# Beginning weight pairs two at a time, in one PSUM bank a pair, and more of them

## The chip, the cores and the metric

The kernel runs on one core of one Trainium2 chip. The metric is the device time of one execution in microseconds (us). The engines of the core each take their own instructions in order: PE (TensorE, matrix products), ACT (ScalarE), DVE (VectorE), POOL (GpSimd) and SP (SyncE, which here only issues transfers). Products are written to PSUM, in banks of 128 x 512 floats, and are read from there by ACT and DVE; everything else lies in SBUF.

## The reference, cut to what matters

One layer of a diffusion backbone over 1024 latent tokens and 256 context tokens, with 1024 channels, in float32:

```
x  = x  + 0.5*g1 * swiglu(modulate(rms_norm(x)),  ffn1_w_in, ffn1_w_out)    # first half step
cx = cx + 0.5*g1c* swiglu(modulate(rms_norm(cx)), ffn1_w_in, ffn1_w_out)
hx = modulate(rms_norm(x));  hc = modulate(rms_norm(cx))
bg, cg, vc, q, k, v, gates = split(hx @ w_in)          # the mixers (1024 x 6656)
y  = bg * short_conv(cg * vc)                          # three taps along the tokens
o  = attention(q, [k_ctx, k], [v_ctx, v])              # 8 query heads, 2 key heads
x  = x + g5 * ((sig(gc)*(y @ w_bc) + sig(ga)*(o @ w_ba)) @ w_out)
x  = x + 0.5*g8 * swiglu(modulate(rms_norm(x)), ffn2_w_in, ffn2_w_out)      # second half step
out = rms_norm(x)

swiglu(h, w_in, w_out): a, b = split(h @ w_in, 2);  (silu(a) * b) @ w_out   # 1024 x 5632, 2816 x 1024
```

The two places of this text are the product `hx @ w_in` of the mixers and the product `h @ ffn2_w_in` of the second half step.

## The kernel before, in words

**Products.** Every float32 product is made of three matmuls on a 128 x 128 weight tile and a 128 x 512 tile of activations: both operands are split into a high part, rounded to the type fp32r, and a low part, the rest. ACT makes the high part (a cast), DVE subtracts it for the low part: this is `split` (lines 197 to 203). The three matmuls are high x high, high x low, low x high (`terms`, lines 688 to 693).

**Seven products for eight.** The large products with two column blocks at once, a *pair* of 128 columns each, go through a Strassen-Winograd scheme (class `Winograd`, lines 492 to 792). Activations are halved by channels and by tokens (C0 is the first 512 tokens, C1 the last), weights by rows and by the two columns of the pair. Seven products of half size (four 128-row tiles of depth, so 4 x 3 = 12 matmuls each) replace eight. Products 1 and 2 need only the halves of C0 (tiles named r, kept under `self.r[1]` and `self.r[2]`) and the first column's own weights; their sum is c, the first one alone is u. Products 6, 7, 4, 5 and 3 need sums of halves, so also C1 (`self.r[3]` to `self.r[7]`), and sums of weights, which GpSimd makes (`lefts`, tiles named sum). DVE adds them to u and c step by step (`second`, `third`).

**Norms.** `norm0` (line 530) norms and modulates C0 and writes r[1] and r[2]. `norm1` (line 557) does C1 and makes the differences: for each of four k it runs six tensor operations and five splits on DVE, and seven operations on ACT. It is a generator, run in six steps: the root mean square, its broadcast, and one step for each k.

**Beginning pairs ahead.** C1 is normed last, and PE would stand still in that time. So `start` (line 710) computes products 1 and 2 of the first `n_ahead` pairs beforehand: 9 for the mixers (AH2) and 9 for the second half step (AH3, line 47). For each pair, product 1 goes to a PSUM bank, ACT copies it to u (a tile named uc), a step of `norm1` is run, product 2 goes to another bank, DVE adds it to u for c, and SP stores u and c to DRAM (tiles named ucd), `put_aside`. The main loop fetches them again one pair ahead (`fetch`), and goes on with products 6, 7, 4, 5 and 3. A pair that wasn't begun has all seven products in the main loop. For a begun pair the weights of its first column are loaded once more in the main loop, for the sums.

**Buffers.** PSUM: five banks for these products (`ps_s`). SBUF: three tiles for raw weights ("raw"), four for split weights ("wl"), four under the tag "wh", which the uc tiles of `start` and the weight sums of the main loop share (`W_BUFS`), eleven small ones for u, c, v, b and the like.

**Look-ahead.** `left` (line 684) makes sure before each product that four split weights are ready or queued in the program (`prefetch`), and takes the first.

**The order of the work.** The program's order is not the order of an engine's queue. The framework plans each engine's order when the kernel is built: an instruction is put in its queue when the planner's own model has its inputs and its buffer ready, the earlier in the program first. Only instructions pinned by hand (`pinned`, `strict`) keep their place. On the chip each engine then waits for whatever stands at the head of its queue.

**Around the change.** For the mixers, `mix.prefetch(4)` and `mix.start(norm1)` stand after the row products of the first half step (lines 1324 to 1329); the main loop over the columns (lines 1346 to 1369) then mixes products with the convolution on DVE, the norm of the context (`normc2`) and the modulation (`mix_steps`). For the second half step, `fast.start(fast.norm1())` stands at line 1816, followed by the loop over 22 pairs.

Of the kernel before, what the change touches and what calls it, by code (L numbers as in the profile page):

```python
# [9 lines left out]
F32 = mybir.dt.float32  # L10
# [8 lines left out]
P = 128  # L19
# [19 lines left out]
W_BUFS = 4  # L39
# [4 lines left out]
WAIT = 4  # L44
AH1, BY_HALF, WARM = 13, 8, 32
TOKENS_AT = 5
RESIDENT, AH2, AH3 = 2, 9, 9
SLOT = 1024


# [1 line left out]
def tile_dit_layer(  # L52
# [44 lines left out]
    act, dve, pool, pe, sp = (Engine(e) for e in (nc.scalar, nc.vector, nc.gpsimd, nc.tensor, nc.sync))  # L97
# [3 lines left out]
    wpool = ctx.enter_context(tc.tile_pool(name="wpool", bufs=5))  # L101
# [7 lines left out]
    def uniq(s):  # L109
        n_tiles[0] += 1  # L110
        return f"{s}_{n_tiles[0]}"

    def atile(name, shape=(P, SLOT), dt=F32):
        return apool.tile(list(shape), dt, tag="A", name=uniq(name))
# [8 lines left out]
    def ps_s(n=512):  # L123
        return psum.tile([P, 512], F32, tag="s", name=uniq("ps"), bufs=5)[:, :n]
# [7 lines left out]
    def matmul(out, w, x, start, stop, pinned=False, on=False):  # L132

        inst = pe.matmul(out, w, x, start=start, stop=stop, skip_group_check=on)
        if pinned:
            tc.keep_in_program_order(inst)
# [49 lines left out]
    def col(name, k=0):  # L186
        o = voff[name] + k
        return cols[:, o : o + 1]
# [36 lines left out]
    def load_cols(w, o, lo_eng=None, pinned=False):  # L225

        return load_w(w[:, o : o + P].rearrange("(k p) n -> p k n", p=P), (KD, P), lo_eng, pinned)

    def mm3(ps, terms, k0=0, k1=None):

        last = len(terms) - 1
        for i, (wh, wl, xh, xl) in list(enumerate(terms))[k0:k1]:
            matmul(ps, wh, xh, start=(i == 0), stop=False)
            matmul(ps, wh, xl, start=False, stop=False)
            matmul(ps, wl, xh, start=False, stop=(i == last))
# [230 lines left out]
    def run(steps, n=None):  # L466

        if n is None:
            for _ in steps:
                pass  # L470
        else:
            for _ in range(n):
                next(steps, None)
# [18 lines left out]
    class Winograd:  # L492
# [192 lines left out]
            self.prefetch(4)  # L685
            return self.ready.pop(0)

        def terms(self, ps, w, i, k):
            r = self.r[i][k]
            wh, wl = (w[:, v, k * P : (k + 1) * P] for v in range(2))  # L690
            matmul(ps, wh, r[:, 0], start=k == 0, stop=False)
            matmul(ps, wh, r[:, 1], start=False, stop=False)
            matmul(ps, wl, r[:, 0], start=False, stop=k == 3)

        def product(self, i):
            w, ps = self.left(), ps_s()
# [12 lines left out]

        def start(self, norm):  # L710

            for i in range(self.n_ahead):
                t = wpool.tile([P, 2, 512], F32, tag="wh", name=uniq("uc"), bufs=W_BUFS)
                u, c = t[:, 0], t[:, 1]
                act.copy(out=u, in_=self.product(1))
                run(norm, 1)
                dve.tensor_add(out=c, in0=u, in1=self.product(2))
                self.put_aside(t)
            run(norm)
            self.fetch()  # L720

# [369 lines left out]
    for k in range(4):  # L1091
        if k % 2:
            half1.shifted(h0[k][:, 0], k, xh[k])
        else:
            dve.tensor_scalar(
                out=h0[k][:, 0], in0=xh[k], scalar1=gain1["l"][:, k : k + 1], scalar2=modl[:, k : k + 1],
                op0=ALU.mult, op1=ALU.add,
            )
        half1.keep(1, k, h0[k][:, 0])
    start = half1.start_by_half()  # L1100
    run(start, 1)
    for k in range(4):
        xt = turned(t0, k + 4, ps_o if k % 2 else ps_t)
# [46 lines left out]
    def all_later_mods():  # L1150
        yield from later_mod(1, (1,), (1,))
        yield from later_mod(0, (0, 1), (1,))
        part_gain(gain1["c"], 0, "g1", "c", 0, 8)
        for _ in normc:
            yield
        for m in range(2, 5):
            yield from later_mod(m)

    steps = all_later_mods()
# [66 lines left out]
    for j in range(NH):  # L1226
        half1.side = side(j) if j >= SIDE_FROM else None
        u, c = half1.next_first()
# [117 lines left out]
    for i in range(KD):  # L1346
        u = atile("u")
# [5 lines left out]
        for ch, bg, gc in mixed():  # L1353
# [4 lines left out]
            for j in (0, 2):  # L1358
# [3 lines left out]
                    out=ya, in0=u[:, a + j - 1 : b + j - 1], scalar=col(f"w{j}", i), in1=ya, op0=ALU.mult, op1=ALU.add  # L1362
# [325 lines left out]
    u = units[0]  # L1688
# [57 lines left out]
    for ch in (C0, C1):  # L1746
        o = ch[1]
        for d in range(KD):
            w = load_cols(w_out[0], d * P)
            load(xs(d, ch), xd[d, :, o : o + 512])  # L1750
            ps = ps_s()
# [4 lines left out]
                out=xs(d, ch), in0=ps, scalar=modl[:, 40 + d : 41 + d], in1=xs(d, ch), op0=ALU.mult, op1=ALU.add  # L1756
# [12 lines left out]
        out=gf[:], in0=cols[:, voff["gf"] : voff["gf"] + 8], scalar1=math.sqrt(D), scalar2=None, op0=ALU.mult  # L1769
# [47 lines left out]
    for j in range(NH):  # L1817
        if j > 1:
            run(last_steps, 3)
        u, c = fast.next_first()  # L1820
# [82 lines left out]
```

## Time and profile before

| | |
|---|---|
| median of three runs | 2644.59 us (2644.15 to 2645.6) |
| the profiled execution: time | 2648.45 us |
| its span, first to last instruction | 2646.7 us |
| granted TensorE clock, mean | 0.994 |
| busy: PE, DVE, ACT, POOL | 2620.2, 2019.7, 1173.9, 549.7 us |
| matmuls | 12665 |

The rows below are from the profile of that execution. "out<-in" names the tiles that an instruction writes and reads; all instructions stand under line 90, where a helper issues them, so they are told apart by tiles. The end of a matmul in the profile is modelled, so a busy PE isn't PE at its peak: counts of matmuls in a stretch of time say more. A number behind "<-" is the idle time of an engine and what ended it.

### The profile page before, as it was taken

How to read it: one execution, taken by the hardware profiler on the slowest of the kernel's cores; microseconds unless marked ns; L12 is line 12 of the kernel's file. 1: busy time of each engine (PE TensorE's matmuls, PEld its weight loads, DVE VectorE, ACT ScalarE, POOL GpSimd, SP SyncE). 2: the span in 40 equal slices, each digit the busy share in tenths (PEclk: the TensorE clock that was granted, in tenths of full speed). 3: DMA queues.
4: the chain of work that ended last, by engine and by line, in shares of the span. 5: the costliest groups of instructions: out<-in, count | busy, mean ns of one | idle time of the engine just before them, and what ended most of it. 6: DMA issues, size and time to landing. Idle time of an engine off the chain costs nothing.

```text
span 2646.7 us, 35358 instructions
## 1 busy us (share of the span) xinstructions
PE 2620.2 (99%) x12665; PEld 2180.4 (82%) x12665; DVE 2019.7 (76%) x3382; ACT 1173.9 (44%) x2321; POOL 549.7 (21%) x425
## 2 busy tenths in 40 slices
PE   8999999999999999999999999999999999999998
PEld 6888898888888777888888888888887888888888
DVE  5888876888897898877788676685457876666996
ACT  6533454433554632333355576674235333334553
POOL 0144101221010044332023112141001442321100
PEclk9999999999999999999999999999999999999999
DMA  8666465335973455242522532123525542327831
GB/s 322 203 211 195 140 214 168 113 120 204 319 170 115 136 171 169 98 133 78 204 73 91 88 88 64 33 49 105 161 81 178 185 155 86 98 76 281 197 84 64
DMA packets 367018, 378.40 MB, mean 143 GB/s; under 512 B 19431, under 2 KB 252025, under 8 KB 366841
## 3 DMA queue, kind: packets, MB, share of 16 engines
q1 hardware_dynamic: 357400, 357.22, 41.7%
q0 software_dynamic: 9440, 18.91, 4.3%
q8 instruction: 99, 1.62, 0.3%
q14 instruction: 79, 0.64, 0.1%
HBM read 306.26 MB, written 69.76 MB: 142 GB/s over the span
## 4 chain that ended last, share of the span: by engine, by line
PE 59%; DVE 2%; ACT 1%; issue 1%; DMA 0%; POOL 0%; SPq 0%; DVEq 0%; ACTq 0%; POOLq 0%
PE ps L90 49%; PE po L90 5%; PE pt L90 5%; DVE xb L90 0%; DVE y L90 0%; DVE r L90 0%; DMA c<-ucd 0%; DVE wl L90 0%; DVE rs_t L90 0%; ACT r L90 0%; DVE wc L90 0%; ACT pts L90 0%; POOL sum L90 0%; DVE pts L90 0%; ACT q L90 0%
## 5 line engine op out<-in xcount | busy, mean ns | idle before, releaser
L90 PE MATMUL ps<-r,wl 128*128 128x512 f32 x5196 | 1208.1, 392 | 10.8 <-DVE r L90 4.8
L90 PEld LDWEIGHTS ps<-r,wl 128*128 128x128 f32 x5196 | 976.0, 189 | 220.7 <-DVE r L90 6.7
L90 ACT CAST wl<-raw 128x512 fp32r<-128x512 f32 x287 | 177.7, 619 | 235.9 <-PE ps L90 189.2
L90 ACT CAST wl<-sum 128x512 fp32r<-128x512 f32 x218 | 134.2, 620 | 301.5 <-PE ps L90 244.9
L90 DVE TENSOR_TENSOR wl<-raw,wl 128x512 fp32r<-128x512 f32 x287 | 209.3, 731 | 62.2 <-ACT wl L90 60.8
L90 POOL TENSOR_TENSOR sum<-raw 128x512 f32<-128x512 f32 x55 | 81.0, 1472 | 657.1 <-DMA raw<-in_w_in_dram 208.5
L90 DVE TENSOR_TENSOR wl<-sum,wl 128x512 fp32r<-128x512 f32 x218 | 194.6, 894 | 23.2 <-ACT wl L90 22.0
L90 DVE TENSOR_TENSOR u<-u,ps 128x512 f32<-128x512 f32 x186 | 126.1, 679 | 39.2 <-PE ps L90 39.1
L90 DVE SCALAR_TENSOR_TENSOR macc<-rawm,silu_c,macc 128x512 f32<-128x512 f32 x178 | 144.5, 830 | 10.3 <-DMA rawm<-in_w_mod_dram 9.9
L90 POOL TENSOR_TENSOR sum<-raw,sum 128x512 f32<-128x512 f32 x55 | 79.0, 1437 | 323.5 <-DVE wl L90 318.0
L90 ACT CAST rh<-hid 128x512 fp32r<-128x512 f32 x132 | 82.0, 622 | 135.2 <-PE ps L90 108.1
L90 DVE TENSOR_TENSOR pts<-pt,pts 128x512 fp32r<-128x512 f32 x160 | 108.6, 686 | 42.5 <-ACT pts L90 40.6
L90 ACT CAST pts<-pt 128x512 fp32r<-128x512 f32 x160 | 93.3, 594 | 86.3 <-PE pt L90 82.6
L90 DVE TENSOR_REDUCE m<-ps 128x1 f32<-128x512 f32 (+1 forms) x192 | 110.2, 594 | 24.3 <-PE ps L90 20.1
L90 PE MATMUL ps<-rh,wl 128*128 128x512 f32 x360 | 122.8, 390 | 0.0
L90 PE MATMUL ps<-wh,r 128*128 128x512 f32 x384 | 120.7, 392 | 0.0
L90 ACT CAST wh<-raw 128x512 fp32r<-128x512 f32 (+1 forms) x85 | 68.0, 801 | 101.3 <-PE ps L90 79.2
L90 DVE TENSOR_TENSOR rl<-hid,rh 128x512 fp32r<-128x512 f32 x132 | 89.9, 684 | 27.0 <-ACT rh L90 18.2
L90 PE MATMUL po<-pts,vh 128*128 128x512 f32 x256 | 110.0, 435 | 0.2 <-ACT pts L90 0.2
L90 PE MATMUL ps<-kl,qs 128*128 128x512 f32 x384 | 104.1, 395 | 0.0
L90 PE MATMUL ps<-rh,wh 128*128 128x512 f32 x300 | 102.8, 389 | 0.0
L90 PE MATMUL ps<-y,wc 128*128 128x512 f32 x384 | 97.1, 392 | 0.2 <-DVE g L90 0.2
(318 smaller groups left out, 5080.8 us busy)
## 6 DMA issues: line engine op xcount, KB each, us to landing
raw<-in_ffn_w_in_dram SPq DMA_DIRECT2D x130, 512.0 KB
raw<-in_ffn_w_out_dram SPq DMA_DIRECT2D x72, 512.0 KB
raw<-in_w_in_dram SPq DMA_DIRECT2D x61, 512.0 KB
rawm<-in_w_mod_dram SPq DMA_DIRECT2D x104, 256.0 KB
hid<-hd SPq DMA_DIRECT2D x40, 512.0 KB
rawm<-in_w_mod_dram SPq DMA_DIRECT2D x32, 512.0 KB
ucd<-uc SPq DMA_DIRECT2D x29, 512.0 KB
ws<-in_ffn_w_out_dram POOLq DMA_DIRECT2D x26, 512.0 KB, 6.4
```

The costliest lines, as they stand in the source:

```text
L90: inst = getattr(self.engine, name)(*args, **kw)
```

## The change

`start` takes the pairs two at a time. For each two it takes four split weights, one PSUM bank and one uc tile a pair. It runs product 1 of both, copies both banks to u on ACT, runs two steps of `norm1`, then adds product 2 of both onto the same banks (the first matmul does not start a new sum) and copies both banks to c on ACT; DVE's add is gone. Both pairs are then stored. For the first two pairs the matmuls go tile by tile, one tile of depth for both pairs and then the next; for later ones, one pair after the other. Twelve pairs are begun for the mixers and ten for the second half step. The first half step has its own `start_by_half`, which is not changed.

```diff
-RESIDENT, AH2, AH3 = 2, 9, 9
+RESIDENT, AH2, AH3 = 2, 12, 10
...
-        def terms(self, ps, w, i, k):
+        def terms(self, ps, w, i, k, begins=True):
             r = self.r[i][k]
             wh, wl = (w[:, v, k * P : (k + 1) * P] for v in range(2))
-            matmul(ps, wh, r[:, 0], start=k == 0, stop=False)
-            matmul(ps, wh, r[:, 1], start=False, stop=False)
-            matmul(ps, wl, r[:, 0], start=False, stop=k == 3)
+            matmul(ps, wh, r[:, 0], start=begins and k == 0, stop=False, on=not begins)
+            matmul(ps, wh, r[:, 1], start=False, stop=False, on=not begins)
+            matmul(ps, wl, r[:, 0], start=False, stop=k == 3, on=not begins)
...
         def start(self, norm):
-            for i in range(self.n_ahead):
-                t = wpool.tile([P, 2, 512], F32, tag="wh", name=uniq("uc"), bufs=W_BUFS)
-                u, c = t[:, 0], t[:, 1]
-                act.copy(out=u, in_=self.product(1))
-                run(norm, 1)
-                dve.tensor_add(out=c, in0=u, in1=self.product(2))
-                self.put_aside(t)
+            for j in range(0, self.n_ahead, 2):
+                n = min(2, self.n_ahead - j)
+                self.prefetch(2 * n)
+                ws, ps = [self.ready.pop(0) for _ in range(2 * n)], [ps_s() for _ in range(n)]
+                ts = [wpool.tile([P, 2, 512], F32, tag="wh", name=uniq("uc"), bufs=W_BUFS) for _ in range(n)]
+                for i in (1, 2):
+                    steps = [(k, e) for k in range(4) for e in range(n)]
+                    for k, e in steps if j == 0 else sorted(steps, key=lambda s: s[1]):
+                        self.terms(ps[e], ws[2 * e + i - 1], i, k, i == 1)
+                    for e in range(n):
+                        act.copy(out=ts[e][:, i - 1], in_=ps[e])
+                    if i == 1:
+                        run(norm, n)
+                for t in ts:
+                    self.put_aside(t)
             run(norm)
             self.fetch()
```

`on` passes a flag that lets matmuls go on with a sum that was closed before. `prefetch`, `put_aside`, `fetch` and `split` are as they were.

## The prediction

> **What bounds the kernel now.** I read the page's busy line first, then the busy table in stretches of ten microseconds over the two places where `start` runs, then the waits there, the chain of waits, and last the groups of instructions.
>
> ```profile
> PE 2620.2 (99%) x12665; PEld 2180.4 (82%) x12665; DVE 2019.7 (76%) x3382; ACT 1173.9 (44%) x2321; POOL 549.7 (21%) x425
> ...
> PEclk9999999999999999999999999999999999999999
> ```
>
> TensorE sets the time. The chain shows its pace where nothing disturbs it:
>
> ```profile
> 2266.50 182.27 PE ps L90 x804
> ```
>
> 182.27 us for 804 matmuls is 0.2267 us each. A stretch of 10 us at that pace is counted as x46 (44.1, and the ones cut by its edges). So each missing one costs 0.2267 us.
>
> The mixers (columns: stretch, its length, then busy us and count of PE, PEld, DVE, ACT, POOL, then clock, DMA share, GB/s):
>
> ```profile
> 880.00:890.00 10.00, 8.06 (x35) 6.10 (x34) 9.96 (x17) 9.46 (x18) 0.00 (x0) 1.00 0.62 205
> ...
> 920.00:930.00 10.00, 10.00 (x46) 8.29 (x45) 9.92 (x16) 5.68 (x10) 5.52 (x3) 1.00 0.64 203
> 930.00:940.00 10.00, 10.00 (x45) 7.95 (x44) 9.31 (x14) 4.32 (x8) 2.24 (x3) 1.00 0.67 214
> 940.00:950.00 10.00, 7.29 (x21) 5.20 (x20) 9.73 (x11) 3.43 (x7) 5.91 (x4) 0.71 0.45 161
> 950.00:960.00 10.00, 10.00 (x43) 8.17 (x43) 6.62 (x8) 3.94 (x9) 4.31 (x4) 0.95 0.37 107
> ...
> 1000.00:1010.00 10.00, 7.95 (x28) 6.05 (x27) 10.00 (x12) 2.28 (x4) 5.32 (x4) 0.83 0.48 157
> ```
>
> and the second half step:
>
> ```profile
> 2030.00:2040.00 10.00, 10.00 (x46) 8.28 (x45) 8.01 (x14) 2.50 (x5) 6.11 (x3) 1.00 0.88 268
> 2040.00:2050.00 10.00, 8.25 (x25) 4.93 (x24) 8.11 (x12) 8.88 (x16) 3.20 (x3) 0.83 0.60 198
> 2050.00:2060.00 10.00, 9.36 (x39) 7.02 (x39) 9.28 (x11) 4.21 (x8) 4.32 (x3) 1.00 0.36 107
> ```
>
> Missing: 11 at 880 (2.5 us), 25 + 3 at 940 to 960 (6.3), 18 at 1000 (4.1), 21 + 7 at 2040 to 2060 (6.3). Together 19.2 us, and no edit that only moves work can win more. Idle time alone doesn't explain them: at 940 PE was idle 2.7 us but lost 6.3. The rest is the clock:
>
> ```profile
> 945.20:950.90 5.70, 5.70 (x14) 4.45 (x15) 5.13 (x8) 1.66 (x3) 1.66 (x1) 0.50 0.04 14
> ```
>
> What ended the waits, for 870 to 900, 930 to 960, 995 to 1012 and 2030 to 2065:
>
> ```profile
> PE ps L90 <- ACT r L90: 1.1, 1, 1.1
> PE ps L90 <- DVE r L90: 0.8, 1, 0.8
> ```
> ```profile
> PE ps L90 <- DVE r L90: 2.7, 2, 2.0
> ```
> ```profile
> PE ps L90 <- DVE wl L90: 2.0, 1, 2.0
> ```
> ```profile
> PE ps L90 <- ACT r L90: 1.3, 2, 0.7
> PE ps L90 <- DVE r L90: 1.0, 1, 1.0
> ```
>
> The r tiles are the normed halves that `keep` writes. At 880 the first ones (`norm0`) come late. At 940 and 2040 it is the last ones of `norm1`: nine begun pairs don't last until VectorE has made them. At 1000 it is a weight split, in the main loop.
>
> [...]
>
> **The change, part by part.** Matmuls: 12 a product, two products a pair, as before; nothing is added or removed on PE.
>
> The add becomes a copy. In both stages:
>
> ```profile
> L90 ACT COPY uc<-ps x9: 573/587/590, 887.4 to 931.2; 128x512 f32<-128x512 f32 x9
> L90 DVE TENSOR_TENSOR uc<-uc,ps x9: 674/678/687, 891.7 to 935.9; 128x512 f32<-128x512 f32 x9
> ```
>
> VectorE loses an add of 0.68 us per begun pair, ScalarE gets a second copy of 0.59. During `norm1` of the mixers (902 to 946) the groups read:
>
> ```profile
> L90 DVE TENSOR_TENSOR uc<-uc,ps 128x512 f32<-128x512 f32 x6 | 4.1, 678 | 0.1
> ...
> L90 DVE TENSOR_TENSOR wl<-sum,wl 128x512 fp32r<-128x512 f32 x3 | 2.0, 679 | 0.0
> ```
> ```profile
> L90 ACT COPY uc<-ps 128x512 f32<-128x512 f32 x6 | 3.5, 583 | 6.7 <-PE ps L90 6.7
> ```
>
> VectorE is full there (9.9 of 10 from 920), so six adds less end `norm1` 4.1 us sooner. ScalarE is busy 4 to 6 of 10, and before those six copies it stood idle 6.7 us for their products: room for six more.
>
> Twelve pairs instead of nine. `start` covered this:
>
> ```profile
> L90 PE MATMUL ps<-r,wl 128*128 128x512 f32 x220 | 51.2, 391 | 1.9 <-ACT r L90 1.1 <-DVE r L90 0.8
> ```
>
> that is 879 to 933, nine pairs (216 matmuls). Three more pairs are 72 x 0.2267 = 16.3 us, so `start` ends near 949. The last r tile that PE waited for came at
>
> ```profile
> 944.91 34.66 PE L90 MATMUL ps<-r,wl 128*128 128x512 f32 x139 [0.73 <-DVE r L90]
> ```
>
> 944.9, and comes near 941 without the adds. Margin 8 us. The six splits that the three pairs add to VectorE in that time (0.68 each, from the row of three above) take the place of main-loop splits that it did there. I take all of the stall: **-6.3 us**. Bounds: -6.3 and 0.
>
> Ten instead of nine in the second half step. The chain there is longer:
>
> ```profile
> 2033.90 0.09 POOL sum L90
> 2033.98 4.55 issue
> 2038.53 2.53 POOL sum L90 x2
> ...
> 2042.13 2.18 ACT r L90 x4
> ...
> 2049.77 6.31 DVE r L90 x5
> ...
> 2057.50 0.50 PE ps L90
> ```
> ```profile
> ACT wl L90 <- POOL sum L90: 6.3, 1, 6.3
> ...
> DVE wl L90 <- ACT wl L90: 3.7, 1, 3.7
> ```
>
> GpSimd's first sum is late, ScalarE queues a split for it and stands 6.3 us, VectorE stands 3.7 us behind that, and the r tiles behind both come last at 2057.5. `start` there is
>
> ```profile
> L90 PE MATMUL ps<-r,wl 128*128 128x512 f32 x217 | 50.1, 391 | 0.0
> ```
>
> from 1991 to 2042. One pair more is 24 x 0.2267 = 5.4 us of cover; six adds less on VectorE (4.1 by the same price) bring the last r tile to 2053.4, and 2049.7 if its 3.7 us go too, against an end of `start` that moves from 2042 to 2047. PE also has products over the first three tiles to do before it needs the last. I leave 1.5 us of the stall: **-4.8 us**. Bounds: -6.3 and 0.
>
> One bank. The second product now adds onto the first one's bank, so it waits until ScalarE has read it. Between the two stands the other pair's first product, 12 x 0.2267 = 2.7 us, against a copy of 0.59 us that starts when its product ends. No wait, if ScalarE is on time; what is queued behind PE's wait is all of PE. In the first two pairs, tile by tile, both products end three matmuls (0.68 us) apart, so only that much lies over the copy: some 0.3 us with the handovers, at two places: **+0.6 us**. Bounds: 0 and 2 x 1.2, both copies bare. [...]
>
> The first two pairs at 880. PE had 13 matmuls in the first five microseconds, with VectorE and ScalarE full:
>
> ```profile
> 880.00:885.00 5.00, 3.06 (x13) 1.95 (x12) 5.00 (x9) 5.00 (x10) 0.00 (x0) 1.00 0.87 305
> ```
>
> Taking two products tile by tile gives PE six matmuls per r tile instead of three. But before, PE could fill with second products in other banks, and now those need a copy from a ScalarE that is 9.5 of 10 busy. Bounds: -0.6 (the gain of the wait of 0.8 less handovers) and +2.0 (three ScalarE instructions ahead of the copies); I take the middle, **+0.7 us**.
>
> Look-ahead. `left` topped up to four split weights at every product; now four are taken at a time and the next four come, in the program, after both second copies. I cost this at nothing, because the planner moves instructions up: the copy for the ninth pair stands at
>
> ```profile
> 931.23 0.58 ACT L90 COPY uc<-ps 128x512 f32<-128x512 f32 x1
> ...
> 938.45 0.62 ACT L90 CAST r<-nt 128x512 fp32r<-128x512 f32 x1 [5.41 <-DVE nt L90]
> ```
>
> 931.2, ahead of casts of `norm1`'s last tile at 938.5, which the program runs in the sixth pair. The cover is the other three products of the two pairs, 8.2 us. Its price without cover is rival two.
>
> Stores and loads. Four more begun pairs cost four more weight loads, stores and reloads of 512 KB, 6 MB in all, on a DMA 0.36 to 0.88 busy in the stretches above. Stores of a couple leave together on SP's queue, ahead of later weight loads, and hold "wh" slots that GpSimd's sums want. With two of four slots for the last couple, two are left for the sums of the first main pair as before: nothing.
>
> Main loop. A begun pair has five products (13.6 us) and not seven, and VectorE saves only two splits and one add (2.0 us) of its own; three more pairs run in that regime. One such stretch stalled (4.1 us at 1000, VectorE 10.00 of 10), later ones did not:
>
> ```profile
> 1060.00:1070.00 10.00, 10.00 (x46) 8.28 (x45) 10.00 (x17) 4.10 (x7) 0.90 (x1) 1.00 0.18 68
> 1070.00:1080.00 10.00, 10.00 (x46) 8.29 (x45) 10.00 (x14) 2.46 (x6) 6.25 (x4) 1.00 0.59 185
> ```
>
> Bounds: -4.1 (the stall at 1000 goes too) and +8.2 (two more). I take 0.
>
> Sum: -6.3 - 4.8 + 0.6 + 0.7 = **-9.8 us**. The profiled execution had a span of 2646.7 and a time of 2648.45 us, 3.9 above the median of 2644.59 of the runs; its own time would be 2638.7. Against the median the forecast is 2634.8 us.
>
> **The rivals.** One: the stalls move into the main loop. VectorE is nearly full in the stretches at 1060 and 1070 and only just kept up; with three more short pairs it falls behind twice at the price of 1000, 2 x 4.1: -9.8 + 8.2 = -1.6, or 2643.0. For it: the stall at 1000 was VectorE's, and the change doesn't touch it. Against: the stretches quoted above, full and without a loss.
>
> Two, the slower side: the look-ahead is lost. At each handover from couple to couple PE then stands for a copy (0.59), a cast (0.62), a split (0.68) and some 0.4 of handovers, 2.3 us. Nine handovers (five and four) are 20.7 us: -9.8 + 20.7 = +10.9, or 2655.5. From 1.1 us a handover it decides the sign. For it: the program's order, and ScalarE's 6.3 us stand behind GpSimd, which would now hold up PE directly. Against: the copy at 931.2.
>
> Three, better: the stall at 1000 goes as well, because VectorE, freed of adds, does context work earlier: -9.8 - 4.1 = -13.9, or 2630.7. For it: the 3.4 us that VectorE was idle at 950 to 960, so it can be moved. Against: nothing in that stretch is edited.
>
> **How the numbers follow.** Forecast 0.50, rival one 0.22, two 0.14, three 0.14. The range takes the forecast with its bounds and leaves out rival two and the far end of the gain: 2627 to 2648 us. About 0.2% (5.3 us) is what a measurement of this kernel can tell. Faster is three, nine tenths of the forecast and a third of rival one (one stall instead of two): 0.14 + 0.45 + 0.07 = 0.66. Slower is rival two, 0.14. The rest is the same, 0.20.
>
> **What would show it.** Stretches after the start of the mixers (some 68 us after its first product) and of the second half step (some 56) with x46 and clock 1.00; VectorE's adds uc<-uc,ps gone but for the 19 of the first half step; 44 copies uc<-ps in the two stages, with PE waits on "ACT uc" under 1 us in all. It is wrong if PE waits on "ACT uc" or "DVE wl" at every second pair, if the clock falls to 0.5 between couples, or if the loss at 1000 is found again twice later.

## The result, and the profile after

The changed kernel takes 2635.99 us (2635.45 to 2638.0), the kernel before beside it 2645.35: a ratio of 0.9963, interval 0.9953 to 0.9972, or 9 to 10 us less. The forecast was 2634.8. The profiled execution of after has a time of 2635.99 and a span of 2634.2, 12.5 us less time than the profiled one of before.

The same rows after: the busy line, then the mixers and the second half step in stretches of ten microseconds (columns as before).

```profile
PE 2610.4 (99%) x12665; PEld 2174.7 (83%) x12665; DVE 1999.2 (76%) x3360; ACT 1182.1 (45%) x2343; POOL 543.5 (21%) x425
```
```profile
880.00:890.00 10.00, 7.55 (x31) 5.25 (x31) 10.00 (x17) 9.48 (x18) 0.00 (x0) 1.00 0.63 207
...
930.00:940.00 10.00, 10.00 (x46) 8.29 (x45) 8.21 (x14) 6.60 (x13) 0.00 (x0) 1.00 0.96 303
940.00:950.00 10.00, 10.00 (x46) 8.29 (x45) 3.10 (x5) 4.62 (x9) 4.87 (x4) 1.00 0.77 271
950.00:960.00 10.00, 10.00 (x46) 8.29 (x45) 6.01 (x8) 3.58 (x10) 4.43 (x4) 1.00 0.50 158
...
1000.00:1010.00 10.00, 10.00 (x45) 8.27 (x45) 10.00 (x14) 3.02 (x5) 5.03 (x4) 1.00 0.50 156
1070.00:1080.00 10.00, 9.51 (x43) 7.55 (x42) 10.00 (x13) 4.05 (x7) 4.43 (x3) 1.00 0.56 184
...
2040.00:2050.00 10.00, 10.00 (x46) 8.26 (x45) 6.49 (x9) 3.12 (x6) 3.79 (x3) 1.00 0.71 247
2050.00:2060.00 10.00, 10.00 (x46) 8.29 (x45) 7.22 (x11) 4.07 (x7) 4.61 (x4) 1.00 0.43 134
```

Both stalls that the change was costed on are gone whole, with the clock at 1.00, and the one at 1000 is gone too (x45 for x28). PE's waits over the whole kernel (total us, times, longest) show what came in their place:

```profile
PE ps L90 <- ACT uc L90: 1.8, 2, 1.1
PE ps L90 <- DVE wl L90: 1.8, 3, 1.0
```

The first is the wait for a copy out of the shared bank: once in the row at 880 (x31 for x35), once in the second half step. The second holds three short waits for weight splits: the longest, 1.0 us, is in the row at 880 as well, another in the row at 1070 (x43 for x46).

Counted as the prediction counted, 0.2267 us a matmul, the rows give: 28 more at 940 to 960, -6.3; 17 more at 1000, -3.9; 28 more at 2040 to 2060, -6.3; four fewer at 880, +0.9; three fewer at 1070, +0.7; the second copy wait (1.8 - 1.1), +0.7. Together -14.2. The profiles differ by 12.5, so 1.7 us were lost in places that these rows don't show; 1.5 of them lie between the two places (the thousand matmuls from 1473 us on), in a stretch where the two profiles of the kernel before also differ, by 1.1. And the profiled execution of before was 3.1 us over the median of its runs (2648.45 against 2645.35), that of after was the median itself: -12.5 + 3.1 = -9.4.

### The profile page after: what moved, and what is told of

Read it like the earlier page. It is cut to its first block, busy times and chain, and to the rows that moved or that the text cites. A ratio compares the mean times of both kernels' runs of the same rounds, so it can differ in the third digit from the quotient of the medians.

```text
span 2634.2 us, 35370 instructions
## 1 busy us (share of the span) xinstructions
PE 2610.4 (99%) x12665; PEld 2174.7 (83%) x12665; DVE 1999.2 (76%) x3360; ACT 1182.1 (45%) x2343; POOL 543.5 (21%) x425
## 4 chain that ended last, share of the span: by engine, by line
PE 93%; DVE 3%; ACT 2%; DMA 1%; issue 1%; SPq 0%; DVEq 0%; ACTq 0%
PE ps L90 78%; PE po L90 8%; PE pt L90 7%; DMA rawm<-in_w_mod_dram 1%; DVE macc L90 1%; DVE xb L90 0%; DVE wl L90 0%; ACT x L90 0%; DMA xtok<-in_x_dram 0%; DVE y L90 0%; ACT r L90 0%; ACT pl L90 0%; DVE u L90 0%; ACT pts L90 0%; ACT wl L90 0%
```

## The experiments

The question was which part of the change brings this: the counts (twelve and ten pairs), the order (two at a time, the first two tile by tile), or the one bank. The theory on record is cover: nine pairs end before `norm1` has made its last r tile, twelve don't. The rival is that the new start earns it, by taking adds from VectorE. Every ratio is to the kernel before, run beside it.

| kernel | start | pairs | median us | ratio (interval) |
|---|---|---|---|---|
| after | new | 12, 10 | 2635.99 | 0.9963 (0.9953 to 0.9972) |
| after, again | new | 12, 10 | 2636.42 | 0.9963 (0.995 to 0.9976) |
| e1_counts | old | 12, 10 | 2635.36 | 0.9955 (0.9942 to 0.9967) |
| e8_counts, again | old | 12, 10 | 2634.83 | 0.996 (0.9947 to 0.9973) |
| e11_counts11 | old | 11, 10 | 2633.57 | 0.9947 (0.9933 to 0.996) |
| e10_counts10 | old | 10, 10 | 2638.98 | 0.9969 (0.9958 to 0.9981) |
| e9_before, again | old | 9, 9 | 2647.05 | 1.0002 (0.9993 to 1.0011) |
| e12_pairs11 | new | 11, 10 | 2640.73 | 0.9974 (0.9964 to 0.9985) |
| e3_pairs129 | new | 12, 9 | 2638.57 | 0.9964 (0.9951 to 0.9976) |
| e4_pairs910 | new | 9, 10 | 2640.22 | 0.9971 (0.996 to 0.9982) |
| e2_pairs99 | new | 9, 9 | 2642.41 | 0.9983 (0.9974 to 0.9992) |
| e6_no_tiles | new, no tile by tile | 12, 10 | 2637.99 | 0.9971 (0.996 to 0.9982) |
| e5_two_banks | new, own bank and add | 12, 10 | 2640.52 | 0.9981 (0.9973 to 0.999) |

**The counts alone**, in the kernel before; and the same again, beside the whole change again.

```diff
-RESIDENT, AH2, AH3 = 2, 9, 9
+RESIDENT, AH2, AH3 = 2, 12, 10
```

> The kernel before with 12 and 10 begun pairs and nothing else: one pair at a time, two banks, VectorE's add kept. Theory A (cover is what pays, the add is a small help): the stall at 940 to 950 of the mixers is gone but VectorE ends norm1 some 4 us later than in the changed kernel; in the second half step one pair more covers 5.4 of the 6.3 us; the loss at 1000 stays. 7 to 10 us faster than before. Theory B (the add taken off VectorE, or the new order of two pairs, is what pays): the stalls only move along, within 3 us of before.

> The kernel before with 12 and 10 alone, again, beside the changed kernel. Theory A: faster than the changed kernel by the two waits for ScalarE's copy, some 2 us less half a us of its own wait at 2051. Theory B: the first run's lead of 2 us was noise, within 1 us.

> The changed kernel again, as the measure for the other three of this call: 9 to 10 us faster than before.

Measured: 2635.36 and 2634.83, against 2635.99 and 2636.42 for the whole change. The new start isn't needed for the gain: the counts alone are no slower. They gain more than theory A of e1_counts has (11.8 us beside the same runs of before, not 7 to 10), and the loss at 1000, which it kept, is gone. Whether they are also faster than the whole change stays open: 1.6 us between the medians run side by side (e8_counts, e7_after), and the runs overlap. PE's waits from 870 to 1010 with the counts alone are those of 880, unchanged from before, and nothing else; below them those from 2000 to 2065:

```profile
PE ps L90 <- ACT r L90: 1.1, 1, 1.1
PE ps L90 <- DVE r L90: 0.8, 1, 0.8
```
```profile
PE ps L90 <- DVE wl L90: 0.3, 1, 0.3
```

**How many pairs**, old start: ten and eleven in the mixers.

```diff
-RESIDENT, AH2, AH3 = 2, 9, 9
+RESIDENT, AH2, AH3 = 2, 10, 10     # e10_counts10; 11, 10 in e11_counts11
```

> The kernel before with ten begun pairs in both stages, nothing else. Cover theory: in the mixers nine pairs end 12 us too early for the last tile's work and leave a wait of some 2.7 us at 943; ten pairs add 5.4 us of matmuls, so the wait at 943 is gone or under 1 us, and the gain is the same as with 12 and 10, 2635 to 2637 us. If the cover needed is more than ten pairs, a wait of 1 to 2 us stays at 943 to 950 and, where the clock falls behind it, the time is 2638 to 2641. The stall at 1004 tells a second thing: if it is left over from the stall at 943, it goes with it; if it depends on the context work being put later by the longer start, it is still there with ten.

> The kernel before with eleven begun pairs in the mixers and ten in the second half step, nothing else. Cover theory: no wait over 0.5 us between 930 and 960, none at 1004, 2635 to 2637 us, the same as with twelve. If each further begun pair costs something in the main loop, eleven is 0.5 to 1 us below twelve, which these rounds hardly tell apart. By the rival theory (the new start, two at a time, is what brings the gain) ten and eleven with the old start stay above 2640.

Ten leave a wait, later and on something else, and end in the range set for that (2638 to 2641). Two lines of PE's waits over the whole kernel, ten pairs:

```profile
PE ps L90 <- ACT wl L90: 2.0, 1, 2.0
PE ps L90 <- DVE wl L90: 2.0, 3, 1.1
```

The first stood at 951, for the main loop's first weight sums; one of the others at 977; none at 1004. Eleven leave none, at 940 or at 1000 (stretches of e11_counts11):

```profile
940.00:950.00 10.00, 10.00 (x45) 8.26 (x44) 9.46 (x13) 5.56 (x12) 2.73 (x3) 1.00 0.87 289
950.00:960.00 10.00, 10.00 (x45) 8.26 (x44) 8.86 (x16) 3.33 (x7) 6.16 (x4) 1.00 0.32 100
...
1000.00:1010.00 10.00, 10.00 (x46) 8.29 (x45) 10.00 (x13) 2.48 (x5) 6.36 (x4) 1.00 0.58 181
```

So the cover that matters lies between ten and eleven pairs: every run of eleven (2632.1 to 2634.4) lies below every run of ten (2637.5 to 2641.6). Eleven with the old start has the lowest median of all, below the 2635 to 2637 expected, but its interval overlaps those of twelve and of the whole change.

**The new start with other counts.** Nine and nine is the new start alone; 12, 9 and 9, 10 split the counts by stage; 11, 10 begins the eleventh pair alone.

```diff
-RESIDENT, AH2, AH3 = 2, 12, 10
+RESIDENT, AH2, AH3 = 2, 9, 9       # e2_pairs99; 12, 9; 9, 10; 11, 10 in the others
```

> The changed kernel with 9 and 9 begun pairs: two at a time, one bank, ScalarE's copy, the ninth pair alone. Theory A: the cover is too short, PE still waits for r tiles near the end of both starts, only the 4 us that the adds cost VectorE are won at each: 4 to 8 us faster than before, and slower than the changed kernel by 3 us or more. Theory B: within 2 us of the changed kernel (9.4 us faster than before).

> The changed kernel with 12 begun pairs in the mixers and 9 in the second half step. Theory A: the mixers are as in the changed kernel; in the second half step the ninth pair ends 5.4 us sooner, and PE waits up to 3 us for r tiles there. 6 to 10 us faster than before. Theory B: the count in the second half step does nothing, 9.4 us faster than before.

> The changed kernel with 9 begun pairs in the mixers and 10 in the second half step. Theory A: the stall at the end of the mixers' start is 2 us or more again, the small stall at 1079 of the changed kernel (0.7 us, a weight split, in the three pairs more) goes; 5 to 8 us faster than before. Theory B: as the changed kernel, 9.4 us faster. If the loss at 1000 of the kernel before is VectorE's alone and not a matter of the count, it comes back here (4 us).

> The changed kernel with eleven begun pairs in the mixers instead of twelve (ten in the second half step as it is); the eleventh pair is begun alone, its product 2 directly behind its own product 1 in the same bank. Odd-pair theory (the 4.7 us wait of the changed start with nine pairs came from the pair that stands alone, whose copy and weight splits nothing covers): a wait of 2 to 5 us of TensorE on a weight split is back near 947 us, with half-rate matmuls behind it, and the time is 2638 to 2642. Cover theory (nine pairs were simply too few): no wait over 1 us between 930 and 1010, and 2635 to 2637, so that the old start with eleven (2633.6, nothing in its way) is lower by the two copy waits alone, some 2 us.

The new start alone brings 4.8 us (2642.41 against 2647.19, the runs of before beside it), well under half of what the counts alone bring beside the same runs (11.8). Theory A of e2_pairs99 has the time right, but not the wait: PE waits for weight splits there, not for r tiles. The new start makes a stall of its own where a pair stands alone. PE's waits from 930 to 965 with nine pairs, and the stretch:

```profile
PE ps L90 <- ACT wl L90: 4.3, 1, 4.3
```
```profile
930.00:940.00 10.00, 5.70 (x19) 4.27 (x18) 9.32 (x13) 5.78 (x11) 2.21 (x2) 0.73 0.56 194
```

ScalarE's order in time shows why (start, length, what; idle before it):

```profile
928.74 0.59 ACT L90 COPY uc<-ps 128x512 f32<-128x512 f32 x1 [1.68 <-PE ps L90]
932.94 0.62 ACT L90 CAST r<-nt 128x512 fp32r<-128x512 f32 x1 [3.62 <-DVE nt L90]
...
935.55 0.58 ACT L90 COPY uc<-ps 128x512 f32<-128x512 f32 x1
936.02 1.14 ACT L90 CAST wl<-sum 128x512 fp32r<-128x512 f32 x2
```

The ninth pair's second copy and the main loop's first weight casts stand in ScalarE's queue behind casts of `norm1`, for which it waits 3.6 us; PE has nothing else left. So with nine pairs two things come together: the last pair stands alone, and `norm1` isn't done. With eleven, too, the last pair is bare (PE, then ScalarE, of e12_pairs11):

```profile
944.37 3.02 PE L90 MATMUL ps<-r,wl 128*128 128x512 f32 x12 [0.68 <-ACT uc L90]
948.58 1.71 PE L90 MATMUL ps<-r,wl 128*128 128x512 f32 x6 [1.19 <-ACT wl L90]
```
```profile
947.42 0.59 ACT L90 COPY uc<-ps 128x512 f32<-128x512 f32 x1 [3.11 <-PE ps L90]
947.91 1.14 ACT L90 CAST wl<-sum 128x512 fp32r<-128x512 f32 x2
```

PE waits 0.7 us for the copy of the pair's own first product, then 1.2 us for a weight split that ScalarE took up only after the second copy. The wait came back as the odd-pair theory has it, though smaller (1.2 us on a split, not 2 to 5) and without half-rate matmuls (clock 1.00 at 940 and at 950). Eleven pairs: old start 0.9947, new start 0.9974, and the intervals don't meet. "Nine were too few" can't explain that alone. But the two waits at the lone pair are 1.9 us, and the two ratios lie some 7 us apart (0.0027): where the rest goes isn't shown, and the profiled execution (2644.25) is the slowest of its eight. Against the new start with twelve, eleven is 2.9 us slower by the ratios, with intervals that overlap. The new start with ten in the mixers, which would tell an odd count from a small one, wasn't run.

Its time is in the odd-pair theory's range (2638 to 2642). By stage: one pair fewer in the second half step (12, 9) leaves a wait of 1.7 us there, on a weight split and not on an r tile as expected, and costs 0.3 us by the ratios; nine in the mixers (9, 10) costs 2.1, and its stall is the 4.3 us of nine and nine. In both the intervals overlap that of after. With 9, 10 the small wait at 1079 is gone, as theory A of e4_pairs910 has it, and the loss at 1000 doesn't come back.

**One bank, or two with the add**, and **without tile by tile**.

```diff
                 for i in (1, 2):
+                    if i == 2:
+                        ps = [ps_s() for _ in range(n)]
...
-                        self.terms(ps[e], ws[2 * e + i - 1], i, k, i == 1)
+                        self.terms(ps[e], ws[2 * e + i - 1], i, k)
...
-                        act.copy(out=ts[e][:, i - 1], in_=ps[e])
+                        if i == 1:
+                            act.copy(out=ts[e][:, 0], in_=ps[e])
+                        else:
+                            dve.tensor_add(out=ts[e][:, 1], in0=ts[e][:, 0], in1=ps[e])
```
```diff
-                    for k, e in steps if j == 0 else sorted(steps, key=lambda s: s[1]):
+                    for k, e in sorted(steps, key=lambda s: s[1]):
```

> The changed kernel (two at a time, 12 and 10) but product 2 goes to a bank of its own and VectorE adds it to u, as before. Theory A (now: the counts pay, the one bank costs two waits of PE for ScalarE's copy, 1.3 and 0.9 us in the changed kernel's trace): no PE wait on ACT uc, no stall at the end of either start; 1 to 3 us faster than the changed kernel. Theory B (the add taken off VectorE is needed): norm1 ends 4 us later and PE waits for r tiles again, 2 us or more slower than the changed kernel.

> The changed kernel without tile by tile: the first two pairs are traced one after the other like the rest. Theory A: the planner puts the first products of the mixers tile by tile in any case, so the waits at 880 to 888 stay within 0.3 us; in the second half step PE waits less for the copies; within 1 us of the changed kernel. Theory B: tile by tile pays at the start of the mixers, 1.4 us or more are lost there.

With two banks the copy waits are gone as expected, but the time is 4.1 us above that of e7_after, run beside it, not below: theory B has the time right, though PE doesn't wait for r tiles. PE's waits, whole kernel, e5_two_banks:

```profile
PE ps L90 <- DVE wl L90: 3.4, 4, 1.1
...
PE ps L90 <- ACT wl L90: 2.0, 1, 2.0
```

They went to weight splits: 5.4 us on wl here, where after has 1.8. That doesn't cover 4.1 us, and this profiled execution (2637.32) is the fastest of its eleven; the other ten all lie above the five of e7_after. So within the new order the one bank with ScalarE's copy is worth more than the 1.8 us that it costs in copy waits; the experiment takes back both at once and doesn't say which of them it is. In the old order the adds do no harm that shows. Without tile by tile the time is 1.6 us higher, inside the intervals. At 880 the waits are the same, as theory A of e6_no_tiles has it; in the second half step the copy wait is 2.0 us for 0.7, where it expected less. PE's waits, whole kernel, e6_no_tiles:

```profile
PE ps L90 <- ACT uc L90: 3.2, 2, 2.0
```

**The kernel before, profiled again.**

> The kernel before, profiled a second time. By the theory that its losses are set by the order of the work, the same four gaps come back at the same places (near 881, 943, 1004 and 2046 us), with waits within 0.3 us of the first profile's; what may differ is how many matmuls after each run at half rate (13, 7 and 4 in the first profile), since its runs spread from 2642 to 2652 us while kernels without those waits spread from 2633 to 2638. If the half-rate matmuls come back in the same counts, the clock is no part of that spread. By the rival theory the gap at 1004 was one execution's accident (a late transfer) and is missing here. Time within 0.2% of the kernel before.

The four gaps are back at their places, 1 to 4 us later (stretches of e9_before):

```profile
940.00:950.00 10.00, 7.21 (x27) 5.28 (x26) 9.89 (x12) 4.41 (x9) 6.11 (x4) 0.90 0.68 244
950.00:960.00 10.00, 10.00 (x42) 8.13 (x42) 6.95 (x10) 3.57 (x9) 5.28 (x4) 0.93 0.38 108
1000.00:1010.00 10.00, 7.66 (x25) 5.87 (x26) 10.00 (x12) 2.27 (x5) 6.06 (x4) 0.83 0.54 180
2040.00:2050.00 10.00, 7.84 (x30) 4.80 (x29) 6.29 (x9) 7.06 (x12) 4.54 (x4) 1.00 0.64 205
```

So the stall at 1000 was no accident of one execution. What ends the wait at 947 differs (a weight split, before it an r tile), by more than the 0.3 us expected, and so does the clock: 0.90 and 0.93 where the first profile had 0.71 and 0.95, and 1.00 at 2040 where it had 0.83.

## Why the prediction was right, and where it wasn't

The time came out 1.2 us above the forecast; 0.8 of that is the base, since the median of the kernel before moved from 2644.59 to 2645.35 with more runs. That the gains agree so closely (9.8 and 9.4) is in part luck: errors of several us cancel.

- **Mixers, -6.3:** right, all of it. The last begun pair's copy starts at 949.6 and the last r tile at 941.0, against "near 949" and "near 941". The 941 fits by luck: the last subtraction for an r tile started at 948.2 before (944.9 is the last one that PE waited for), so it came 7.2 us sooner, where the adds were to bring 4.1; see GpSimd, below. Nor is a shorter `norm1` needed: with eleven pairs under the old start the same subtractions take 38.0 us from first to last, against 39.0 before and 32.0 after, and PE waits for none of the last ones.

```profile
L90 DVE TENSOR_TENSOR r<-nt,r x16: 678/683/1773, 908.9 to 946.9; 128x512 fp32r<-128x512 f32 x16
```

- **Second half step, -4.8:** under-sized; the rows give the whole 6.3. The subtractions for the r tiles there (durations min, median, max; first and last start), before and after:

```profile
L90 DVE TENSOR_TENSOR r<-nt,r x16: 678/681/1779, 2018.1 to 2057.5; 128x512 fp32r<-128x512 f32 x16
```
```profile
L90 DVE TENSOR_TENSOR r<-nt,r x16: 677/684/693, 2005.3 to 2036.7; 128x512 fp32r<-128x512 f32 x16
```

They take 31.4 us from first to last instead of 39.4. That is 8.0 us sooner, the prediction's larger case (2049.7 for 2057.5, both savings); the value taken, -4.8, allowed for less. But the stall goes without that too. With the counts alone, adds and all, they take 38.5 us, and PE waits 0.3 us in all:

```profile
L90 DVE TENSOR_TENSOR r<-nt,r x16: 678/694/1014, 2009.8 to 2048.3; 128x512 fp32r<-128x512 f32 x16
```

So the 5.4 us of matmuls that the tenth pair adds were cover enough for waits of 2.3 us, and the 1.5 us left standing were too cautious.

- **Stall at 1000, 0:** wrong; 3.9 us went, which was rival three's outcome and a stated bound. Its mechanism, adds taken from VectorE, isn't what did it alone: with the counts alone the adds remain and the stall goes as well. It went in every variant, with ten or more pairs under the old start and with nine under the new one, though in three of them (e10_counts10, e5_two_banks, e12_pairs11) PE waits 0.8 to 1.1 us for a weight split somewhat earlier, between 970 and 990. VectorE is as full in that stretch as before (10.00 of 10 with eleven pairs), so it is ahead of PE rather than less loaded; which work it then has behind it was not isolated, and stays open.
- **One bank, +0.6:** right in kind, under-sized: 1.8 us in two waits, where "under 1 us in all" had been claimed. Together with **the first pairs, +0.7**, 1.3 were forecast; the rows give 0.9 at 880, the first copy wait included, and 0.7 in the second half step, 1.6. At 880 the waits for r tiles fell from 1.9 us to 0.4, but beside the 1.1 for the copy came 1.0 for a weight split, which the prediction didn't have.
- **Look-ahead, 0:** right for twelve and ten only. Rival two's handover (copy, cast, split, PE bare) is real, but at one place, the pair that stands alone; e2_pairs99 and e12_pairs11 show it. The even counts tried under the new start, twelve and ten, don't have one.
- **Main loop, 0:** the two more stalls of rival one didn't come; one new wait at 1070 cost 0.7.
- **The sum against the median:** -9.8 was summed from a profile that lay 3.9 us over the median, and taken off the median unchanged. From there to the measured -9.4: -3.9 at 1000, -1.5 in the second half step, +0.3 for one bank and first pairs, +0.7 at 1070, +1.7 elsewhere, and +3.1 by which the profiled execution was dearer than the median run. The missed 3.9 at 1000 and this 3.1 offset each other, and nothing joins the two. The last section has what the clock's part in that surplus may be.
- **The clock at 940:** the 3.6 us put down to it (6.3 lost, 2.7 idle) are too many. Of the 6.3, 13 matmuls 0.43 us apart instead of 0.2267 make 2.6. By this count the remaining 3.7 are waiting; the profile, in which the ends of matmuls are modelled, shows 2.7 of them as idle time. The sum doesn't use it.
- **The range, 2627 to 2648:** its lower end is the sum of all lower bounds (-17.3), so the far end of the gain is in it, not left out; the upper bounds add up to +12.6, or 2657, and for 2648 no working is given.

What the prediction couldn't see is that most of the change isn't needed: it costed the new start as a small loss (+1.3) and the counts as the gain. At twelve and ten pairs the runs agree, within their noise; at nine and nine the new start gains 4.8 us. But it also put the adds (4.1 us each stage) down as a cause of the gain. The counts alone, adds and all, gain as much.

## What to carry to other kernels

Where an engine works ahead to cover another's serial stage, set the amount first, one step at a time, before rewriting how the work is begun: here ten, eleven and twelve pairs gave 0.9969, 0.9947 and 0.9955. A rewrite in groups of two wants an even count: here the odd pair alone showed the copy and the weight split that a couple hides (0.7 and 1.2 us with eleven pairs). And price a stall from several executions, not one: the clock's part, 2.6 of the 6.3 us lost at 940 in one profile, differed in the next (clock 0.71 in the first ten microseconds, then 0.90).

## What the runs showed of the hardware

**Beside GpSimd's sums a subtraction of VectorE took up to 1.77 us, clear of them at most 0.69.** The same subtraction of `norm1` (durations min, median, max; first and last start), in before and in after:

```profile
L90 DVE TENSOR_TENSOR r<-nt,r x16: 678/682/1772, 909.2 to 948.2; 128x512 fp32r<-128x512 f32 x16
```
```profile
L90 DVE TENSOR_TENSOR r<-nt,r x16: 681/686/689, 909.0 to 941.0; 128x512 fp32r<-128x512 f32 x16
```

In before GpSimd begins the main loop's sums while `norm1` still runs (busy 5.52 of 10 at 920, 2.24 at 930, 5.91 at 940), and single subtractions take up to 1.77 us; in after it is idle until 940 and none takes over 0.69. The second half step's pair of rows, above, reads the same: 1.78 and 0.69. In the profile of before, over both places (900 to 960 and 2000 to 2065), 14 of VectorE's two-input operations (TENSOR_TENSOR, 128x512) that read SBUF alone take over 0.7 us, and all 14 run beside a GpSimd instruction; the 63 that run clear of one take at most 0.69, and so do the 18 with an input in PSUM that run beside one. The uc tiles of the added pairs hold the "wh" slots that the sums want: in after GpSimd stands idle for 150.0 us, in two waits, before its sums, and what ends them is the store of a uc tile; in before no sum waits for one. From 930 to 946 the group read x7 at 1145 ns in before; with the counts alone and with ten pairs:

```profile
L90 DVE TENSOR_TENSOR r<-nt,r 128x512 fp32r<-128x512 f32 x7 | 5.6, 818 | 0.0
```
```profile
L90 DVE TENSOR_TENSOR r<-nt,r 128x512 fp32r<-128x512 f32 x8 | 8.9, 1137 | 0.7 <-ACT r L90 0.7
```

So beginning twelve pairs also shortened the work that they cover; with ten that had not yet set in, and with eleven (917 ns) only in part. That the uc tiles alone hold the sums back wasn't tried; with eleven pairs GpSimd is idle at 920 as well (0.00 of 10, for 5.52 in before), and no sum waits for a uc tile between 870 and 1000.

**Behind two waits the clock read 0.59 in one profile, and 1.00 behind equal ones.** The two waits at 880 are the same in the kernel before and with eleven pairs under the old start (1.1 and 0.8 us of idle time in both). The 4 us that follow aren't; before, then e11_counts11:

```profile
883.20:887.20 4.00, 3.97 (x17) 3.30 (x18) 4.00 (x8) 4.00 (x8) 0.00 (x0) 1.00 0.38 131
```
```profile
881.30:885.30 4.00, 3.99 (x11) 3.11 (x12) 4.00 (x8) 4.00 (x8) 0.00 (x0) 0.59 0.38 127
```

Of four profiles read there (before twice, the old start with ten and with eleven pairs) only this one has the lower clock, and 11 matmuls in the 4 us where before has 17; the other three have 1.00. At 2040 the kernel before had four matmuls 0.43 us apart in one profile (clock 0.83) and none in the other (1.00). Around the 4.3 us wait of nine pairs (e2_pairs99) the clock was 0.73 in the ten microseconds from 930 and 0.93 in the next. Among the ten runs of e9_before those at a mean granted clock of 0.995 took 2648.2 to 2650.3 us, those at 0.997 2645.0 to 2645.6; the profiled one of before had 0.994. So the length of a wait didn't settle whether the clock fell behind it: 1.1 and 0.8 us had both outcomes. What did settle it, no run here shows.
